# A two-layer decoder trunk on one core: modulation sums on VectorE, negated attention scores, and the gate row applied at the accumulators

## The chip, the cores and the metric

The kernel runs on one core of a Trainium2 chip. A core has TensorE (matmuls, into PSUM), VectorE, ScalarE, GpSimd and SyncE (which only issues transfers here); each works through its own queue in order. In the rows they are PE (and PEld for the loading of weights), DVE, ACT, POOL and SP. The metric is the device time of one execution in microseconds (us); less is better.

## The reference, cut to what matters

Two layers, 512 tokens, 1024 channels, all in f32. A layer is a modulated RMS norm, a token mixer, a residual add, a second modulated norm and a mixture of 16 experts with another residual add. The mixer of layer 0 is an mLSTM, that of layer 1 is differential attention with 8 heads.

```
c_act = silu(c)
mod = c_act @ w_ada[l] + b_ada[l]            # 1024 x 6144 per layer; sh1, sc1, g1, sh2, sc2, g2
h = rms(x, norm1[l]) * (1 + sc1) + sh1
y = mixer(h)                                  # projections, mixing, then @ w_out
x = x + g1 * y
...
# attention: for each head two score matrices of queries against keys
q = rope(rms(q, q_norm)) * 64 ** -0.5
p = softmax(where(mask, q @ k.T, -inf))       # p[0], p[1]
a = p[0] - lam * p[1]
```

## The kernel before, in words

Work is written as a program for each engine; a scheduler with a model of the times sets each engine's order before the run, save where the text ties it (`issue_after`, `ordered`). `later(n, fn)` puts work n steps ahead in a queue that `step()` runs.

**Modulation parts.** The 12 parts of `mod` (6 per layer) need w_ada, 4 MB per part. Layer 0's shift and scale for the first norm come from TensorE (`ada_half`). Six more parts, four of layer 0 and the first two of layer 1, come from `ada`, interleaved with the first mixer's projections: each part is four 1 MB transfers into a ring of four buffers (tag `raw`) that the projection weights share. A transfer holds two row blocks of 128 x 1024. Of a part's eight blocks the first is scaled on ScalarE (L255). In layer 0's parts blocks 2, 4 and 6 are multiplied and added in one VectorE operation (L257). All others are scaled in place on ScalarE (L259) and added on GpSimd (L260). `column_sums` then turns the sum (PE L301, DVE L302), and L307 writes `mod`. The last four parts of layer 1 use TensorE (`ada_rows`, L280).

**Weights in two parts.** Each projection weight block is split: a rounded high part on ScalarE (L228) and the low rest on VectorE (L229); for the first strips of the two mixers, `qk0` and `b00`, the rest is made on GpSimd. Every product is three TensorE matmuls. There are two buffers for low parts and three for high ones.

**Output projection.** `out_proj` runs for tokens 0 to 255 (half 0), then 256 to 511 (half 1), over the same four w_out buffers. In half 0 each accumulator is multiplied by the gate row g1 (L499) and added to x (L500). In half 0 GpSimd also multiplies each weight block by g1 in place (L512), after its split, and half 1 splits the product, so half 1 only adds. After `out_proj` of half 1 comes the route to the experts (squares, L366/L367, transposes, router logits L1087, ranks), then the experts, whose weights arrive in 1 MB transfers.

**Scores.** `scores` (L905 on) makes one 128-query block of one head: two matmuls (L917), a VectorE operation that adds the mask and takes the row maximum (L920), a tiny VectorE product with -0.125 (L923), the exponential on ScalarE (L924), the reciprocals and the factor of the second matrix (L927, L928), its scaling (L929) and the sum (L930).

**From layer 0 to layer 1.** The last expert's result is added to x by L1616, eight operations for the four token blocks. `normed_T` of layer 1 squares x on ScalarE (L373) and takes 1/rms from L366 on VectorE and L367 on GpSimd.

## Time and profile before

| what | value |
|---|---|
| median of 3 runs | 1228.6 us (1227.84 to 1230.41) |
| profiled execution | 1225.23 us |
| its span | 1223.4 us |
| TensorE busy | 1126.9 us, 92% |
| VectorE busy | 808.9 us, 66% |
| ScalarE busy | 659.1 us, 54% |
| GpSimd busy | 307.7 us, 25% |
| mean granted TensorE clock | 0.952 |

The span is that of the profiled execution; 1.83 us of its time lie outside it. The busy share is a mean over stages: start and first mixer until about 257 us, the end of its output projection and the route until 310, the experts of layer 0 until 582, attention until about 880, its route until 945, and the experts of layer 1.

### The profile page before, as it was taken

What the parts mean: (1) busy time and instruction counts of PE and PEld (TensorE: products, weight loads), DVE (VectorE), ACT (ScalarE), POOL (GpSimd) and SP (SyncE); (2) the same over time, 40 slices, a digit from 0 to 9 for tenths busy, and PEclk for the clock granted to TensorE, in tenths of its full rate; (3) what the DMA queues carried; (4) which work ended last, traced back from release to release, by engine and by line L of the source; (5) the groups of instructions that cost most, each with busy time, mean ns of one, the idle gap of its engine ahead of it and who ended that gap; (6) DMA issues with size and microseconds to landing.
All of it is one profiled execution on the core that took longest, in us unless ns stands there. A gap on an engine that the chain in (4) does not pass through costs nothing.

```text
span 1223.4 us, 17320 instructions
## 1 busy us (share of the span) xinstructions
PE 1126.9 (92%) x5954; PEld 816.0 (67%) x5954; DVE 808.9 (66%) x1617; ACT 659.1 (54%) x1118; POOL 307.7 (25%) x245
## 2 busy tenths in 40 slices
PE   5999999988999999996899999978797999999976
PEld 3677777777787875332897877757586787774322
DVE  4566878887888995006856566675677899893024
ACT  3456675443788885112655555555553888883110
POOL 2555482462211111101211021223233211111100
PEclk8999999997999999998999999988896999999998
DMA  9788662195799999999124444411275899999994
GB/s 345 267 284 302 230 216 104 59 346 194 280 383 382 386 380 368 398 408 370 37 70 141 138 169 138 173 69 74 99 280 193 316 386 385 377 380 372 396 414 182
DMA packets 104172, 320.81 MB, mean 262 GB/s; under 512 B 12673, under 2 KB 25097, under 8 KB 103056
## 3 DMA queue, kind: packets, MB, share of 16 engines
q1 hardware_dynamic: 95120, 298.67, 65.8%
q0 software_dynamic: 8960, 20.99, 4.7%
q8 instruction: 49, 0.80, 0.3%
q14 instruction: 43, 0.35, 0.1%
HBM read 309.66 MB, written 20.97 MB: 270 GB/s over the span
## 4 chain that ended last, share of the span: by engine, by line
PE 70%; DMA 12%; DVE 11%; ACT 4%; issue 2%; POOL 1%; SPq 0%; DVEq 0%; POOLq 0%; ACTq 0%
PE pge L237 8%; PE pue L237 8%; PE pge L1339 6%; PE po L237 6%; DMA we<-in_moe_w_gu_dram 5%; DMA ada<-in_w_ada_dram 5%; PE py0e L237 4%; PE py1e L237 4%; PE pye L1366 3%; PE s L917 3%; PE pcf L1398 2%; PE o L949 2%; PE xTe L427 1%; PE rowada L280 1%; PE psr L1087 1%
## 5 line engine op out<-in xcount | busy, mean ns | idle before, releaser
L1339 PE MATMUL pge<-we,xfe 128*64 128x512 f32 x448 | 106.3, 616 | 19.2 <-DMA we<-in_moe_w_gu_dram 19.2
L260 POOL TENSOR_TENSOR acc<-acc,ada 128x1024 f32<-128x1024 f32 x30 | 80.8, 2694 | 54.8 <-ACT ada L259 22.2
L1348 DVE TENSOR_TENSOR acte<-acte,pge 128x256 f32<-128x256 f32 x14 | 5.9, 421 | 119.3 <-ACT acte L1347 119.3
L1311 POOL DMA_INDIRECT xg<-h2d,lstd x26 | 26.8, 1031 | 223.0 <-PE xTe L427 152.5
L1339 PEld LDWEIGHTS pge<-we,xfe 128*64 128x64 f32 x448 | 30.4, 141 | 74.4 <-issue 51.1
L367 POOL TENSOR_TENSOR qrs<-qrs,nhalf 128x4 f32<-128x4 f32 x32 | 35.5, 1111 | 154.9 <-DVE qrs L366 126.5
L1366 PE MATMUL pye<-we,aTe 128*64 128x512 f32 x224 | 50.6, 593 | 1.1 <-ACT aTe L1355 1.1
L259 ACT ACTIVATE ada<-ada,cact 128x1024 f32<-128x1024 f32 x30 | 33.8, 1145 | 31.0 <-DMA ada<-in_w_ada_dram 31.0
L924 ACT ACTIVATE p<-p,mx 128x128 f32<-128x128 f32 (+3 forms) x64 | 35.7, 559 | 23.7 <-DVE mx L923 23.6
L920 DVE CUSTOM_DVE_ANT_0 p<-s,maskW 128x128 f32<-128x128 f32 (+3 forms) x64 | 30.4, 487 | 26.6 <-ACT orow L951 14.3
L512 POOL TENSOR_TENSOR wo<-wo,grow 128x1024 f32<-128x1024 f32 x16 | 40.9, 2573 | 23.6 <-DVE wos102l L229 15.8
L1347 ACT ACTIVATE acte<-pge 128x256 f32<-128x256 f32 x14 | 5.4, 383 | 73.1 <-PE pge L1339 73.1
L917 PE MATMUL s<-kTb,qTb 64*128 64x128 f32 (+3 forms) x128 | 40.1, 503 | 2.9 <-DVE mx L920 2.2
L1366 PEld LDWEIGHTS pye<-we,aTe 128*64 128x64 f32 x224 | 16.0, 137 | 32.3 <-issue 29.6
L427 PE MATMUL xTe<-ident,xg 128*128 128x128 f32 x144 | 23.0, 290 | 5.8 <-POOL we L220 3.2
L1463 POOL DMA_INDIRECT yd<-yoe,lstd x12 | 14.7, 1227 | 52.0 <-ACT yoe L1558 51.3
L949 PE MATMUL o<-vb,aTs 128*128 128x128 f32 x160 | 26.1, 303 | 0.7 <-ACT aTs L941 0.7
L1378 ACT ACTIVATE yo<-pye,twins 128x512 f32<-128x512 f32 x8 | 5.5, 687 | 38.9 <-PE pye L1366 38.9
L367 POOL TENSOR_TENSOR ors<-ors,nhalf 128x2 f32<-128x2 f32 (+1 forms) x12 | 11.2, 930 | 58.8 <-DVE mx L923 39.5
L949 PEld LDWEIGHTS o<-vb,aTs 128*128 128x128 f32 x160 | 23.2, 214 | 3.0 <-ACT aTs L941 1.6
L1379 POOL DMA_INDIRECT yd<-yo,rows x8 | 8.0, 1001 | 65.7 <-ACT yo L1378 65.4
L427 PEld LDWEIGHTS xTe<-ident,xg 128*128 128x128 f32 x144 | 18.5, 149 | 8.2 <-issue 6.0
(2557 smaller groups left out, 3871.5 us busy)
## 6 DMA issues: line engine op xcount, KB each, us to landing
we<-in_moe_w_gu_dram SPq DMA_DIRECT2D x128, 1024.0 KB, 8.7
we<-in_moe_w_down_dram SPq DMA_DIRECT2D x64, 1024.0 KB, 8.9
ada<-in_w_ada_dram SPq DMA_DIRECT2D x48, 1024.0 KB, 5.5
we<-yd SPq DMA_DIRECT2D x8, 1024.0 KB, 18.3
wo<-in_a_w_out_dram SPq DMA_DIRECT2D x4, 1024.0 KB, 4.9
wo<-in_b_w_out_dram SPq DMA_DIRECT2D x4, 1024.0 KB, 4.9
x<-in_x_dram SPq DMA_DIRECT2D x4, 512.0 KB, 5.0
qk0w<-in_a_w_in_dram SPq DMA_DIRECT2D x2, 1024.0 KB, 14.7
```

What stands on the lines that cost most here:

```text
L237: T.matmul(ps, (xh, xh, xl)[i], w, start=first and i == 0, stop=last and i == 2)
L259: A.activation(raw[:, k], raw[:, k], AF.Copy, scale=cact[:, kt:kt + 1])
L260: G.tensor_tensor(acc, acc, raw[:, k], op=ALU.add)
L367: pows.append(G.tensor_tensor(r, r, nhalf[:, 0:ncol], op=ALU.pow))
L427: T.transpose(ps[:, k * P:(k + 1) * P], row[:, kt * P:(kt + 1) * P], ident)
L512: G.tensor_tensor(raw[:, k], raw[:, k], grow, op=ALU.mult)
L917: T.matmul(ps[:, 0:n], part(qTs, h)[q0:q0 + BHD, j * P:(j + 1) * P], part(kTs, h)[q0:q0 + BHD, 0:n], start=True, stop=True)
L920: V.tensor_tensor_reduce(p[:, 0:n], ps[:, 0:n], maskW[:, S - n:S], scale=1.0, scalar=NEG, op0=ALU.add, op1=ALU.max, accum_out=mx[:, cc:cc ...
L924: A.activation(p[:, 0:n], p[:, 0:n], AF.Exp, scale=0.125, bias=mx[:, cc:cc + 1], accum_out=mx[:, 2 + cc:3 + cc])
L949: T.matmul(po[:, 0:P], aT[:, kb * P:(kb + 1) * P], part(vs, h)[:, kb * P:(kb + 1) * P], start=kb == 0, stop=kb == j)
L1339: T.matmul(pgu[hf * CS:(hf + 1) * CS].rearrange("p (g c) -> p g c", g=2), x[:, kt], w[:, :, hf], start=kt == 0, stop=kt == NK - 1))
L1366: T.matmul(py[hf * CS:(hf + 1) * CS], aT[:, k, ch * CS:(ch + 1) * CS], w[:, 0, hf * 512:(hf + 1) * 512], start=ch + k == 0, stop=ch + k == 2))
```

## The change

- `ada`: every row block but the first is one VectorE operation (L257's form); the ScalarE scaling and the GpSimd add are gone (30 of each).
- `strip`: the low parts of `qk0` and `b00` are made on VectorE.
- `out_proj`: GpSimd no longer multiplies w_out by the gate row (8 operations per layer); both halves multiply the accumulators by it on VectorE (4 operations more per layer).
- Scores: the factor -0.125 goes into the column `wcq` that scales q, so the scores are negated, the mask and the maximum change sign, L923 is gone, and L929 and L930 become one operation.
- Layer seam: the additions of L1616 keep program order, and for token blocks 2 and 3 of layer 1 the VectorE step of 1/rms (L366) is queued behind the last addition.

```diff
--- before.py
+++ after.py
@@ -211,7 +211,7 @@
         G.iota(slot, pattern=[[1, P]], base=0, channel_multiplier=0, **ints)
 
 
-    loads, last, act_last = [], [], []
+    loads, last, act_last, added = [], [], [], []
 
     def load(src, a, n, name, where=None, after=None):
         pool, tag, bufs = where or (raws, "raw", N_RAW)
@@ -253,11 +253,8 @@
                 kt = ch * 2 + k
                 if kt == 0:
                     A.activation(acc, raw[:, k], AF.Copy, scale=cact[:, kt:kt + 1])
-                elif k == 0 and l == 0:
+                else:
                     V.scalar_tensor_tensor(acc, raw[:, k], cact[:, kt:kt + 1], acc, op0=ALU.mult, op1=ALU.add)
-                else:
-                    A.activation(raw[:, k], raw[:, k], AF.Copy, scale=cact[:, kt:kt + 1])
-                    G.tensor_tensor(acc, acc, raw[:, k], op=ALU.add)
             if ch == 3:
                 room[2].append(lambda: ada_sums(l, j, acc))
                 later(3, lambda: room[2] and room[2].pop()())
@@ -371,7 +368,8 @@
 
         ss = small.tile([P, 1], F32, tag="ss", name=f"ss{l}{t}", bufs=4)
         A.activation(junk, xt[t], AF.Square, accum_out=ss)
-        r = rstd_of(ss, 1, D, f"r{l}{t}")
+        with tc.issue_after(added[0].ins) if added and t > 1 else nullcontext():
+            r = rstd_of(ss, 1, D, f"r{l}{t}")
         ps = [bank(f"hT{l}{t}{hf}") for hf in range(2)]
         for kt in range(NK):
             T.transpose(ps[kt // 4][:, kt % 4 * P:(kt % 4 + 1) * P], xt[t][:, kt * P:(kt + 1) * P], ident)
@@ -440,7 +438,7 @@
             raw = load(wk(w[k0 * P:(k0 + 2 * a) * P, col0:col0 + n]), 2 * a, n, f"{name}w{k0}",
                        first and first[k0 // (2 * a)])
             for k in (0, a):
-                yield k0 + k, split(raw[:, k:k + a], a, n, f"{name}s{k0 + k}", G if name in ("qk0", "b00") else V)
+                yield k0 + k, split(raw[:, k:k + a], a, n, f"{name}s{k0 + k}")
                 next(mix, None)
 
     def proj_rows(at, w, col0, evac, name, mix, n=512, by_token=False):
@@ -495,8 +493,7 @@
             if kt == NK - 1:
                 for n in range(2):
                     cols = slice(n * 512, (n + 1) * 512)
-                    if half == 0:
-                        V.tensor_tensor(ps[t, n], ps[t, n], grow[:, cols], op=ALU.mult)
+                    V.tensor_tensor(ps[t, n], ps[t, n], grow[:, cols], op=ALU.mult)
                     V.tensor_tensor(xt[t][:, cols], xt[t][:, cols], ps[t, n], op=ALU.add)
                 done(t)
             step()
@@ -508,8 +505,6 @@
             for k in range(2):
                 kt = ch * 2 + k
                 parts[kt] = split(raw[:, k:k + 1], 1, D, f"wos{l}{half}{kt}")
-                if half == 0:
-                    G.tensor_tensor(raw[:, k], raw[:, k], grow, op=ALU.mult)
                 if kt < NK - 3:
                     for t in ts:
                         products(t, kt)
@@ -834,6 +829,8 @@
             V.memset(wc, 1.0)
             for c0 in (0, BHD):
                 SP.dma_start(wc[c0 + R2:c0 + BHD], w[0:1, R2:].rearrange("o d -> d o"))
+            if nm == "q":
+                V.tensor_scalar(wc, wc, -0.125, None, op0=ALU.mult)
             tab = const.tile([P, NT, 2 * R2], F32, name=f"tab{nm}")
             bc = lambda a: a[:, None, :].to_broadcast([P, NT, ROPE_HALF])
             V.tensor_tensor(tab[:, :, 0:8], cos, bc(wr[:, 0:8]), op=ALU.mult)
@@ -864,7 +861,7 @@
             maskW = pool.tile([P, S], F32, name="maskW")
             G.memset(maskW[:, 0:S - P], 0.0)
             past(maskW[:, S - P:])
-            V.tensor_scalar(maskW[:, S - P:], maskW[:, S - P:], 0.0, NEG, op0=ALU.is_gt, op1=ALU.mult)
+            V.tensor_scalar(maskW[:, S - P:], maskW[:, S - P:], 0.0, -NEG, op0=ALU.is_gt, op1=ALU.mult)
             a1 = scale_of(1, slice(0, 4)) + scale_of(1, slice(4, 8))
             rows = [y_tile(f"rrow1{i}") for i in range(2)]
             for t in range(NT):
@@ -917,17 +914,15 @@
                     T.matmul(ps[:, 0:n], part(qTs, h)[q0:q0 + BHD, j * P:(j + 1) * P], part(kTs, h)[q0:q0 + BHD, 0:n],
                              start=True, stop=True)
                     p = pool.tile([P, S], F32, tag=f"p{cc}", name=f"p{j}{h}{cc}", bufs=3)
-                    V.tensor_tensor_reduce(p[:, 0:n], ps[:, 0:n], maskW[:, S - n:S], scale=1.0, scalar=NEG,
-                                           op0=ALU.add, op1=ALU.max, accum_out=mx[:, cc:cc + 1])
+                    V.tensor_tensor_reduce(p[:, 0:n], ps[:, 0:n], maskW[:, S - n:S], scale=1.0, scalar=-NEG,
+                                           op0=ALU.add, op1=ALU.min, accum_out=mx[:, cc:cc + 1])
                     pr.append(p)
-                    V.tensor_scalar(mx[:, cc:cc + 1], mx[:, cc:cc + 1], -0.125, None, op0=ALU.mult)
-                    A.activation(p[:, 0:n], p[:, 0:n], AF.Exp, scale=0.125, bias=mx[:, cc:cc + 1],
+                    A.activation(p[:, 0:n], p[:, 0:n], AF.Exp, scale=-1.0, bias=mx[:, cc:cc + 1],
                                  accum_out=mx[:, 2 + cc:3 + cc])
                 p0, p1 = pr
                 V.reciprocal(mx[:, 4:6], mx[:, 2:4])
                 V.scalar_tensor_tensor(mx[:, 5:6], mx[:, 5:6], mx[:, 2:3], nlam, op0=ALU.mult, op1=ALU.mult)
-                V.tensor_scalar(p1[:, 0:n], p1[:, 0:n], mx[:, 5:6], None, op0=ALU.mult)
-                V.tensor_tensor(p0[:, 0:n], p0[:, 0:n], p1[:, 0:n], op=ALU.add)
+                V.scalar_tensor_tensor(p0[:, 0:n], p1[:, 0:n], mx[:, 5:6], p0[:, 0:n], op0=ALU.mult, op1=ALU.add)
                 later(5, lambda: probs_T(j, h, p0, mx))
 
             def probs_T(j, h, p0, mx):
@@ -1613,7 +1608,8 @@
                     to_tokens(banks[t], t, *mine, False, True)
                     for hf in range(2):
                         x = xt[t][:, hf * 512:(hf + 1) * 512]
-                        V.tensor_tensor(x, x, banks[t][hf], op=ALU.add)
+                        added[:] = [V.tensor_tensor(x, x, banks[t][hf], op=ALU.add)]
+                        ordered(added[0])
             elif e >= NE - NSEL:
                 selected.append((weighted_few(py, e), places(e)))
             elif e == NE - NSEL - 1:
```

## Rows read from the trace of the kernel before

**Rows 1.** Stages: us, busy of each engine (instructions), PEclk, DMA share, GB/s
```profile
50.00:222.00 172.00, 164.72 (x771) 130.85 (x769) 128.70 (x223) 103.38 (x162) 85.86 (x38) 1.00 0.61 211
222.00:257.00 35.00, 28.50 (x152) 23.57 (x151) 30.55 (x39) 14.11 (x24) 24.36 (x11) 0.95 0.51 196
...
600.00:790.00 190.00, 189.17 (x1412) 155.91 (x1411) 118.80 (x449) 101.61 (x277) 35.40 (x33) 1.00 0.39 134
790.00:880.00 90.00, 74.36 (x390) 55.75 (x389) 61.39 (x175) 50.20 (x134) 28.86 (x17) 0.85 0.25 94
```

**Rows 2.** The expert stage of layer 0, same view and columns
```profile
330.00:470.00 140.00, 139.69 (x642) 110.91 (x641) 126.07 (x125) 117.86 (x138) 24.13 (x20) 1.00 1.01 380
```

**Rows 3.** Groups of instructions, POOL, 20 to 300 us (busy, mean ns, idle before)
```profile
L260 POOL TENSOR_TENSOR acc<-acc,ada 128x1024 f32<-128x1024 f32 x30 | 80.8, 2694 | 54.8 <-ACT ada L259 22.2 <-DVE acc L257 15.2 <-PE o0p L456 5.1
```

**Rows 4.** Groups of instructions, DVE, 28 to 282 us
```profile
L257 DVE SCALAR_TENSOR_TENSOR acc<-ada,cact,acc 128x1024 f32<-128x1024 f32 x12 | 15.4, 1280 | 11.8 <-DMA ada<-in_w_ada_dram 6.5 <-POOL acc L260 5.4
```

**Rows 5.** Timeline of DVE and PE, first mixer: start, us, idle before
```profile
140.68 3.43 DVE L229 TENSOR_TENSOR v1s2l<-v1w,v1s2h 128x1024 fp32r<-128x1024 f32 x1
...
257.32 1.21 DVE L229 TENSOR_TENSOR wos011l<-wo,wos011h 128x1024 fp32r<-128x1024 f32 x1
...
144.16 0.50 PE L455 MATMUL v1p<-v1s2l,ah 128*128 128x512 f32 x1 [1.07 <-DVE v1s2l L229]
```

**Rows 6.** Timeline of POOL, DVE and PE, end of the first mixer
```profile
234.03 21.09 POOL L512 TENSOR_TENSOR wo<-wo,grow 128x1024 f32<-128x1024 f32 x8 [1.21 <-ACT grow L361]
...
240.21 3.38 DVE L229 TENSOR_TENSOR wos007l<-wo,wos007h 128x1024 fp32r<-128x1024 f32 x1
...
244.25 0.66 PE L427 MATMUL ht<-ident,hrow 128*128 128x128 f32 x4 [2.15 <-DVE cs L302]
250.69 1.12 PE L360 MATMUL psrow<-ident,a 128*128 128x128 f32 x4 [3.68 <-DVE swr L1030]
```

**Rows 7.** Timeline of POOL, DVE and PE, end of attention
```profile
814.11 5.24 POOL L512 TENSOR_TENSOR wo<-wo,grow 128x1024 f32<-128x1024 f32 x2
...
814.59 2.56 DVE L891 TENSOR_TENSOR qrow<-qrow,qrs 128x256 f32<-128x256 f32 x1
...
817.19 2.21 DVE L894 TENSOR_TENSOR rot<-qrow,tabk 128x32 f32<-128x32 f32 x1
...
860.60 2.40 DVE L928 SCALAR_TENSOR_TENSOR mx<-mx,nlam 128x1 f32<-128x1 f32 x1
...
820.16 0.66 PE L903 MATMUL qkT<-ident,qrow 128*128 128x128 f32 x2 [4.71 <-DVE mx L928]
...
864.30 1.06 PE L917 MATMUL s<-kTb,qTb 64*128 64x256 f32 x2 [2.19 <-DVE mx L920]
```

**Rows 8.** Groups of instructions, DVE, 600 to 880 us
```profile
L891 DVE TENSOR_TENSOR qrow<-qrow,qrs 128x256 f32<-128x256 f32 x32 | 15.6, 488 | 7.7 <-POOL qrs L367 6.5 <-PE qkT L903 1.2
...
L929 DVE TENSOR_SCALAR p<-p,mx 128x128 f32<-128x128 f32 (+3 forms) x32 | 12.3, 386 | 0.8
...
L923 DVE TENSOR_SCALAR mx<-mx 128x1 f32<-128x1 f32 x64 | 8.4, 147 | 0.3
```

**Rows 9.** Timeline of DVE, last additions of layer 0's projection
```profile
282.47 1.88 DVE L500 TENSOR_TENSOR x<-x,po 128x512 f32<-128x512 f32 x3 [0.60 <-PE po L237]
284.27 1.33 DVE L229 TENSOR_TENSOR guse01l<-we,guse01h 128x1024 fp32r<-128x1024 f32 x1
285.53 0.67 DVE L500 TENSOR_TENSOR x<-x,po 128x512 f32<-128x512 f32 x1
```

**Rows 10.** Timeline of DVE, the seam between the layers
```profile
582.22 0.15 DVE L366 TENSOR_SCALAR r<-ss 128x1 f32<-128x1 f32 x1 [1.27 <-ACT sq L373]
```

**Rows 11.** Timeline of DVE and PE, start of the first projection
```profile
24.74 2.23 DVE L398 TENSOR_SCALAR a<-mod 128x4 f32<-128x4 f32 x1
...
28.46 2.07 PE L479 MATMUL qk0p<-ah,qk0s0h 128*128 128x512 f32 x4 [0.23 <-ACT ah L403]
```

**Rows 12.** Waits of ACT, 50 to 222 us: total us, times, longest
```profile
ACT ada L259 <- DMA ada<-in_w_ada_dram: 22.7, 12, 3.2
```

## The prediction, made before the change was run

> **What bounds the kernel now.** I read the table of stages first, to find where TensorE is idle, then the timelines of TensorE and VectorE at each idle place, then what GpSimd did at that moment.
>
> In the main part of the first mixer TensorE is busy for 164.72 of 172.00 us, and through attention for 189.17 of 190.00 [rows 1]. Work taken from other engines there is mostly work that TensorE already covers. The idle time lies in two short stretches: 6.50 us in the 35 us from 222 to 257, and 15.64 us in the 90 us from 790 to 880 [rows 1]. In the expert stage behind them TensorE is busy for 139.69 of 140 us while the transfers run at a DMA share of 1.01 [rows 2]. Its work starts when the route has chosen the tokens, so I expect what is won before it to shift the rest as a whole.
>
> The timelines show what ends the idle time. A low part takes VectorE 1.21 us when GpSimd is quiet and 3.43 us when it is not, and TensorE then waits 1.07 us for it [rows 5]. For the 21.09 us in which GpSimd multiplies the eight w_out blocks, a low part takes 3.38 us, and TensorE stands for 2.15 and 3.68 us behind small VectorE work that is queued after it [rows 6]. Near the end of attention it is the same: beside two GpSimd products of 5.24 us in all, two VectorE operations take 2.56 and 2.21 us, the second on 32 elements per partition, and TensorE stands for 4.71 us; later one on a single element takes 2.40 us, and TensorE stands for 2.19 us [rows 7]. So GpSimd costs this kernel time by holding up VectorE, not by its own results.
>
> The Trainium skill says why (GPSIMD Engine Reference, Specifications): GpSimd's SBUF interfaces are shared with VectorE, and they contend when a VectorE instruction has two SBUF inputs or runs in a two-port mode. By that rule the added operations, with two SBUF inputs each, also wait whenever GpSimd works, which speaks against them. Beside the GpSimd work that the rows leave in the main part (85.86 us less 28 of the 30 removed adds at 2.694, some 10 us) that would put up to 10 us on VectorE, and the sum would be 10 us smaller if all of it reached TensorE; the trace agrees with the rule itself (2.40 us on one element, in an operation with several inputs), not with such a price, since TensorE's gaps are much shorter than VectorE's stretches.
>
> **The change part by part.** The sum is made against the profiled execution, 1225.23 us (its span 1223.4 and 1.83 around it). The median of the runs is 1228.6, which is 3.37 higher.
>
> *Start of the first projection.* The `qk0` low part held VectorE's 4-element operation for 2.23 us, just ahead of the first projection [rows 11]. But TensorE was on a modulation matmul until 0.23 us before that projection starts [rows 11], and I expect it to keep that order. Bounds: nothing, and the 2.23. I take -0.2, the gap.
>
> *Modulation in the main part.* Removed: 30 GpSimd adds of 2.694 us [rows 3] and 30 ScalarE scalings. Added: 30 VectorE operations at 1.280 [rows 4], 38.4 us, two of them before 50 us. VectorE is busy for 128.70 of 172 us there [rows 1]. With nothing given back it would be at about 165, full; if half of 28 adds stretched an operation by the 2.22 us between 3.43 and 1.21 [rows 5], 31 us come back and it is at 133, as full as before. I take that half, as an estimate. TensorE's idle time in this part is 7.28 us in all [rows 1], so no more can be won; the one gap shown of this cause is 1.07 [rows 5]. I take -2.0, about two such gaps. The other bound is a loss, from waits on the w_ada transfers that move into VectorE's queue, ahead of the low parts that TensorE needs: ScalarE waited 22.7 us for them, in 12 waits [rows 12]. One wait holds up a low part less than the other buffer covers: a block of 1024 columns feeds 24 matmuls, and a release of the buffers no longer waits for GpSimd. So I take no loss.
>
> *Gate row, layer 0.* The eight products of 21.09 us are gone [rows 6]. TensorE's two gaps are 5.83 us together [rows 6], of 6.50 idle in the stretch [rows 1]. Each ends behind VectorE work that was stretched. I take -5.5; bounds nothing and -6.5.
>
> *Gate row, layer 1.* The same eight products go. Of the gap of 4.71 us the two operations at their usual length (0.49 for the first form, mean of 32 [rows 8]) leave about 0.5, so 4.2 come back; the gap of 2.19 goes with the stretch of 2.40 [rows 7]. That is -6.4, and I take -6.5 with the small stretches around. Bounds: -2.2 if only one of the two comes back, and -11, two thirds of the idle 15.64 [rows 1].
>
> *Half 1's four gate products, per layer.* Three additions of a 128x512 accumulator take 1.88 us, 0.63 each [rows 9]; a product of the same shape is priced alike. The last addition now ends at 286.20 (285.53 and 0.67). Eight operations from 282.47 on end at 287.5 if the split of 1.33 us that lies between [rows 9] is put elsewhere, and at 288.8 if not: 1.3 to 2.6 later. Some of it is hidden, since token block 3 queues behind the logits of block 2. I take +1.0 per layer, +2.0; bounds 0 and 5.2.
>
> *Scores.* 64 operations of 147 ns and 32 of 386 ns go [rows 8], 21.7 us of VectorE. Up to 790 us TensorE hides all of it: 0.83 us idle in 190 [rows 1]. If that cover were gone it would be worth up to those 21.7. From 790 on each pair of score blocks has a chain shorter by some 0.5 us, mostly beside other heads. I take -0.5; bounds nothing and -3.
>
> *Seam of the layers.* The additions of block 3 no longer stand behind a 1/rms step that waits 1.27 us for ScalarE [rows 10]. Their accumulators were done only shortly before, so not all of it counts: -0.4; bounds nothing and -1.3. Behind it waits the ScalarE square of block 3. The low parts of `b00` go to VectorE at the end of layer 0, where it is idle: nothing, or +2.4, two at 1.21, if the weighted sum of the last expert is queued behind.
>
> Sum: -0.2 - 2.0 - 5.5 - 6.5 + 2.0 - 0.5 - 0.4 = -13.1. That is 1212.1 us for an execution like the profiled one, and 1215.5 against the median.
>
> **The rivals.**
>
> *VectorE's queue takes the mixer's gain back.* The waits on w_ada stand ahead of the low parts, just enough to cost what the removal of GpSimd's work wins in layer 0. For it: the mixer has 38.4 us more of VectorE work. Against it: GpSimd no longer stretches it. Only layer 1, the seam and the scores count: -6.5 - 0.5 - 0.4 + 2.0 = -5.4, 1223.2 us.
>
> *Slower: VectorE bounds the first mixer.* All 22.7 us of waits [rows 12] move to VectorE and reach TensorE, and the 2.0 of the main part is not won: 1228.6 - 11.1 + 22.7 = 1240.2 us. It decides from 11.1 us on, when half of those waits reach TensorE. For it: at 165 of 172 us VectorE would have no room for them. Against it: ScalarE stood in these waits, made the high parts in the same queue, and TensorE was idle for only 7.28 us.
>
> *Nothing comes of it.* Other waits (ScalarE's copies, the ring of four buffers) end in the same places as the stretched VectorE work: 1228.6 us.
>
> *More comes of it.* All the idle time goes that GpSimd's work could have caused: -7.3 in the main part, -6.5 behind it, -11 at the end of attention, -2 in seam and scores, nothing lost in half 1: -26.8, 1201.8 us.
>
> **How the numbers follow.** Forecast, 1215.5 us: 0.55; its own range is 1209 to 1221, by the bounds of the two gate terms. Gain in layer 1 alone, 1223.2: 0.20. Slower, 1240.2: 0.10. Nothing, 1228.6: 0.07. More, 1201.8: 0.08. Faster by over 0.2% (2.5 us, about what a measurement of this kernel can tell from no change) is 0.55 + 0.20 + 0.08 = 0.83; within it 0.07; slower 0.10. For a range of 8 in 10 I leave out most of the case of more and the slower case: 1205 to 1228.
>
> **What would show it.** Right: no VectorE operation of 2 to 3.5 us beside GpSimd in 222 to 257 and 810 to 866, where TensorE's gaps of 2.15, 3.68, 4.71 and 2.19 us are gone; VectorE busy for about 130 of 172 us in the main part, and TensorE no more idle there; the experts of layer 0 starting some 7 us earlier and those of layer 1 some 13. Wrong: gaps of TensorE behind low parts that wait for a w_ada operation; the four gaps still there behind other work; a last addition of half 1 more than 2.6 us later behind its last matmul than now.

## The result, and the profile after

The changed kernel takes 1219.24 us (median) where the kernel before takes 1229.47: a ratio of 0.990, 95% interval 0.9868 to 0.9932. Run again beside the experiments it took 1215.58 against 1227.51, 0.9904 (0.9876 to 0.9932). The forecast was 1215.5, faster, with a range of 1205 to 1228. The first profiled execution of the changed kernel took 2186.41 us, with matmuls of nearly twice the usual length throughout (1140 ns for 616 in the experts' first product), so the profile after is that of the second measurement (one execution of 1215.05 us, span 1212.9).

I cut both profiles into stages at the same events, read from TensorE's timeline: the first and last matmul of the output projection (`po`), the first transposed expert input (`xTe`), the last matmul of the combination (`pcf`), the first of `b00`, the last of `bv6`. The first fence is the kernel before: first mixer, output projection of layer 0, its tail up to the experts; then the last heads of attention, the output projection of layer 1, its tail. Columns as in [rows 1].

```profile
28.46:211.94 183.48, 175.65 (x819) 135.99 (x820) 127.39 (x217) 106.38 (x158) 94.73 (x53) 0.99 0.68 238
211.94:283.83 71.89, 65.39 (x340) 54.21 (x339) 58.97 (x101) 32.85 (x54) 32.87 (x21) 0.98 0.55 205
283.83:308.31 24.48, 16.14 (x95) 15.50 (x93) 17.74 (x76) 7.25 (x13) 8.61 (x10) 0.58 0.39 148
808.00:836.20 28.20, 17.70 (x96) 13.15 (x95) 17.66 (x46) 16.78 (x42) 6.92 (x4) 0.72 0.11 38
836.20:920.11 83.91, 76.64 (x376) 60.50 (x375) 58.05 (x131) 43.99 (x101) 30.04 (x20) 0.91 0.46 176
920.11:943.23 23.12, 14.66 (x95) 13.94 (x93) 17.40 (x75) 7.16 (x13) 8.42 (x9) 0.63 0.52 198
```

The same six stages of the changed kernel:

```profile
28.29:207.58 179.29, 175.36 (x823) 137.88 (x820) 130.46 (x250) 79.09 (x130) 8.06 (x20) 0.98 0.68 244
207.58:270.71 63.13, 63.13 (x338) 52.94 (x336) 48.14 (x101) 32.37 (x54) 11.22 (x12) 1.00 0.57 226
270.71:298.64 27.93, 17.93 (x96) 16.90 (x95) 19.82 (x79) 7.31 (x13) 9.53 (x10) 0.59 0.41 147
801.40:822.95 21.55, 16.04 (x89) 11.10 (x87) 11.85 (x36) 15.18 (x36) 1.70 (x2) 0.81 0.13 49
822.95:900.56 77.61, 74.02 (x374) 58.53 (x372) 49.05 (x113) 43.39 (x101) 13.67 (x13) 0.94 0.49 190
900.56:928.90 28.34, 18.10 (x95) 17.19 (x95) 20.09 (x81) 6.98 (x13) 8.38 (x9) 0.55 0.42 162
```

The first column after the window is the length; length less PE's busy time is TensorE's idle time. Subtracted, with what the prediction gave for the stage:

```
stage                        change   of it idle   of it TensorE busy   predicted
first mixer                   -4.2       -3.9             -0.3            -2.0
output projection, layer 0    -8.8       -6.5             -2.3            -5.5
tail, layer 0                 +3.5       +1.7             +1.8            +1.0
last heads of attention       -6.7       -5.0             -1.7   } -6.5 and
output projection, layer 1    -6.3       -3.7             -2.6   } -0.5 (scores)
tail, layer 1                 +5.2       +1.8             +3.4            +1.0
```

In the two output projections and the two tails TensorE's instructions are the same in both kernels, but for one or two at the edges. There the idle time that went took TensorE busy time with it, and the idle time that came brought some: the matmuls themselves ran faster or slower. In the last heads it is otherwise. Seven instructions fewer stand in that stage (89 for 96), since the scheduler put them ahead of the end of `bv6`, and they account for the 1.7 us of busy time.

The other stages: start -0.2 (predicted -0.2), experts of layer 0 +1.1, seam (end of `pcf` to `b00`) 6.43 to 7.30, +0.9 (predicted -0.4), attention up to `bv6` +1.1 (it holds those seven instructions), experts of layer 1 274.1 to 278.9, +4.8. The sum of all is -9.5 between the two profiles, up to the last matmul of the combination; the spans differ by 10.5. The experts of layer 0 start 9.7 us earlier and those of layer 1 14.3, where the prediction said some 7 and 13.

What answers to the rows of before. The low part of w_out that took 3.38 us in [rows 6], and the small operation behind it:

```profile
232.74 1.23 DVE L229 TENSOR_TENSOR wos007l<-wo,wos007h 128x1024 fp32r<-128x1024 f32 x1 [0.63 <-PE po L237]
...
234.95 0.17 DVE L304 TENSOR_TENSOR mod<-cs,vcol 128x8 f32<-128x8 f32 x1
```

The gaps of 2.15, 3.68, 4.71 and 2.19 us [rows 6, 7] have no counterpart; from `po` first to `po` last in layer 0 TensorE is busy for 63.13 of 63.13 us. Two VectorE operations of 2.3 us are left in that stage beside GpSimd's L1062 (at 247.82 and 251.88); TensorE waits for neither. The 30 GpSimd adds [rows 3] are gone, and the VectorE group of [rows 4] has 42 members of the same length; its waits for w_ada total 7.3 us:

```profile
L257 DVE SCALAR_TENSOR_TENSOR acc<-ada,cact,acc 128x1024 f32<-128x1024 f32 x42 | 53.9, 1282 | 9.6 <-DMA ada<-in_w_ada_dram 7.3 <-ACT acc L255 1.9 <-DVE wcq L829 0.2
```

New is a wait at the start of the first mixer, where two of these operations stand ahead of the modulation of the second half of the input, and one more ahead of its low parts:

```profile
46.04 1.28 DVE L257 SCALAR_TENSOR_TENSOR acc<-ada,cact,acc 128x1024 f32<-128x1024 f32 x1
...
47.36 1.28 DVE L257 SCALAR_TENSOR_TENSOR acc<-ada,cact,acc 128x1024 f32<-128x1024 f32 x1
...
48.56 1.91 DVE L408 TENSOR_SCALAR xnT<-xnT,a,mod 128x512 f32<-128x512 f32 x4
...
50.67 1.28 DVE L257 SCALAR_TENSOR_TENSOR acc<-ada,cact,acc 128x1024 f32<-128x1024 f32 x1 [0.19 <-DVE wcq L829]
...
51.87 2.49 DVE L402 TENSOR_TENSOR al<-xnT,ah 128x512 fp32r<-128x512 f32 x4
...
49.82 1.72 PE L477 MATMUL qk0p<-ah,qk0s4h 128*128 128x512 f32 x4 [2.27 <-ACT ah L401]
...
52.61 0.80 PE L478 MATMUL qk0p<-al,qk0s4h 128*128 128x512 f32 x1 [0.64 <-DVE al L402]
...
53.20 0.63 PE L479 MATMUL qk0p<-ah,qk0s4l 128*128 128x512 f32 x1
...
53.63 0.63 PE L477 MATMUL qk0p<-ah,qk0s4h 128*128 128x512 f32 x1
...
50.00:57.00 7.00, 6.36 (x15) 4.30 (x16) 6.81 (x14) 2.61 (x4) 0.63 (x4) 0.52 0.63 180
```

TensorE waits 2.27 us, and then its 128x512 matmuls are issued 0.43 us apart. The granted clock from 50 to 57 us is 0.52, the lower level (1.2 of 2.4 GHz) nearly throughout. VectorE's small additions and memsets between them are left out of the fence. The kernel before starts these matmuls 0.23 us apart, at the full clock:

```profile
50.00:57.00 7.00, 7.00 (x32) 5.19 (x30) 6.77 (x9) 3.62 (x5) 5.16 (x4) 1.00 0.54 120
```

In the tail of layer 1 a split of the first expert's weights stands among half 1's products (L496) and additions (L497), and the last addition ends 5.3 us behind the last `po` matmul, where it was 2.4 before ([rows 9] show the additions of layer 0, also 2.4). What follows on TensorE, first in the changed kernel:

```profile
901.60 1.92 DVE L229 TENSOR_TENSOR guse01l<-we,guse01h 128x1024 fp32r<-128x1024 f32 x1
...
904.04 1.87 DVE L497 TENSOR_TENSOR x<-x,po 128x512 f32<-128x512 f32 x3
...
904.77 1.12 PE L1070 MATMUL x2T<-ident,x 128*128 128x128 f32 x4 [2.98 <-DVE x L497]
...
905.96 1.97 PE L1070 MATMUL x2T<-ident,x 128*128 128x128 f32 x8
...
907.72 1.73 PE L1082 MATMUL psr<-awr,x2T 128*128 128x16 f32 x8
...
905.00:912.00 7.00, 6.99 (x38) 6.83 (x37) 6.82 (x20) 4.11 (x8) 3.65 (x5) 0.50 0.68 274
```

and in the kernel before:

```profile
922.55 1.09 PE L1075 MATMUL x2T<-ident,x 128*128 128x128 f32 x8 [1.51 <-DVE x L500]
...
923.48 0.96 PE L1087 MATMUL psr<-awr,x2T 128*128 128x16 f32 x8
...
922.50:926.00 3.50, 3.23 (x30) 3.14 (x30) 3.46 (x8) 2.98 (x6) 3.03 (x3) 0.99 1.02 405
```

The eight transposes of a token block take 1.97 us where they took 1.09, the eight logit matmuls 1.73 where they took 0.96: after a wait of 2.98 us in place of 1.51 TensorE does the same work at a granted clock of 0.50 in place of 0.99.

### The profile page after: what moved, and what is told of

The parts are those of the page before. It is cut to its first block, busy times and chain, and to the rows that moved or that the text cites. A ratio compares the mean times of both kernels' runs of the same rounds, so it can differ in the third digit from the quotient of the medians.

```text
span 2184.5 us, 17129 instructions
## 1 busy us (share of the span) xinstructions
PE 2145.9 (98%) x5954; PEld 1308.0 (60%) x5954; DVE 799.9 (37%) x1566; ACT 651.8 (30%) x1090; POOL 164.3 (8%) x193
## 4 chain that ended last, share of the span: by engine, by line
PE 97%; DVE 1%; DMA 1%; ACT 1%; issue 0%; POOL 0%; SPq 0%; DVEq 0%; POOLq 0%; ACTq 0%
PE pge L1334 10%; PE pge L237 9%; PE pue L237 9%; PE po L237 8%; PE pye L1361 5%; PE py0e L237 5%; PE py1e L237 5%; PE s L914 3%; PE pcf L1393 2%; PE o L944 2%; PE xTe L425 2%; PE rowada L277 1%; PE psr L1082 1%; PE aT L934 1%; PE aTe L1440 1%; PE qk0p L478 1%
## 5 line engine op out<-in xcount | busy, mean ns | idle before, releaser
L1334 PE MATMUL pge<-we,xfe 128*64 128x512 f32 x448 | 213.2, 1140 | 0.0
L1361 PE MATMUL pye<-we,aTe 128*64 128x512 f32 x224 | 108.0, 1158 | 1.1 <-ACT aTe L1350 1.1
L1361 PEld LDWEIGHTS pye<-we,aTe 128*64 128x64 f32 x224 | 22.4, 188 | 80.1 <-issue 78.3
L914 PE MATMUL s<-kTb,qTb 64*128 64x128 f32 (+3 forms) x128 | 62.8, 800 | 0.6 <-ACT kTb L901 0.6
L257 DVE SCALAR_TENSOR_TENSOR acc<-ada,cact,acc 128x1024 f32<-128x1024 f32 x42 | 53.8, 1281 | 6.2 <-ACT acc L255 5.7
L1393 PE MATMUL pcf<-yo,self 64*128 64x512 f32 x96 | 45.4, 1140 | 1.7 <-DVE yo L1367 1.7
L425 PE MATMUL xTe<-ident,xg 128*128 128x128 f32 x144 | 40.2, 442 | 5.8 <-POOL we L220 3.2
L944 PE MATMUL o<-vb,aTs 128*128 128x128 f32 x160 | 44.0, 456 | 0.5 <-ACT aTs L936 0.5
L944 PEld LDWEIGHTS o<-vb,aTs 128*128 128x128 f32 x160 | 40.3, 345 | 6.6 <-issue 4.6
L277 PE MATMUL rowada<-ada,acc 128*32 128x512 f32 x128 | 33.6, 1087 | 0.0
L1082 PEld LDWEIGHTS psr<-awr,x2T 128*128 128x128 f32 x128 | 30.6, 361 | 1.3 <-issue 0.9
```

What stands on the lines that cost most here:

```text
L257: V.scalar_tensor_tensor(acc, raw[:, k], cact[:, kt:kt + 1], acc, op0=ALU.mult, op1=ALU.add)
L277: T.matmul(ps[at:at + 32], cp[:, ch * 2 + k], raw[:, k, hf * 512:(hf + 1) * 512], start=True, stop=True)
L425: T.transpose(ps[:, k * P:(k + 1) * P], row[:, kt * P:(kt + 1) * P], ident)
L914: T.matmul(ps[:, 0:n], part(qTs, h)[q0:q0 + BHD, j * P:(j + 1) * P], part(kTs, h)[q0:q0 + BHD, 0:n], start=True, stop=True)
L944: T.matmul(po[:, 0:P], aT[:, kb * P:(kb + 1) * P], part(vs, h)[:, kb * P:(kb + 1) * P], start=kb == 0, stop=kb == j)
L1082: T.matmul(ps, xT[:, kt], awr[:, kt], start=kt == 0, stop=kt == NK - 1)
```

## The experiments

**The whole change, and two parts of it.** All ten hunks; the gate row alone (the deletion of GpSimd's products and the `if half == 0` of out_proj); the modulation alone (the hunk of `ada`).

Whole change. 

> The changed kernel once more, for a profile in the usual state. Theory (GpSimd costs time by holding up VectorE): 0.985 to 0.993 of before; none of the TensorE gaps of 2.15, 3.68, 4.71 and 2.19 us is left, no VectorE operation of 2 to 3.5 us stands beside the output projections, the first mixer's main part has VectorE at some 130 of 172 us. Rival (VectorE's queue takes the mixer's gain back): the experts of layer 0 start less than 2 us earlier, and new TensorE gaps end behind low parts that waited for a modulation operation.

Measured above: 0.9904.

Gate row alone. 

> Before, with only the gate row moved to the accumulators in both halves. Theory: 7 to 12 us faster than before (5.5 + 6.5 - 2.0 = 10), most of the whole gain. Rival (gain comes from the modulation sums): within 3 us of before.

0.9927 (0.9899 to 0.9955), 1218.0 us. Its stages: output projection of layer 0 63.1, tail 27.8, last heads 23.4, output projection of layer 1 75.5, tail 28.1. So all that layer 1 wins, and the longer tails, belong to the gate row; the last heads lack 1.8 us that the whole change has, and its output projection is 2.1 us shorter.

Modulation alone. 

> Before, with only the modulation row blocks as VectorE operations. Theory: 0 to 4 us faster, TensorE was idle for only 7.28 us in that part. Rival (VectorE bounds the mixer): 5 us or more slower. Rival (the modulation carries the gain): 6 us or more faster.

0.9992 (0.9976 to 1.0007): no change that can be told. The first mixer is 1.6 us shorter (181.9), the tail of layer 0 1.3 (23.2; a second profile of the kernel before, below, shows the same 23.3), and the output projection of layer 1 is 3.1 longer (87.0; why is open). The loss at the start of the mixer is there too, and larger: waits of 2.66 and 1.27 us, and the fourth weight block (`qk0s6`) starts at 61.36, where it starts at 55.60 before and at 59.86 in the whole change.

**Is it the products, or who makes them?** In layer 0, half 0, GpSimd multiplies the eight w_out blocks by the gate row again, into a buffer that nothing reads at that time (`spare` holds it in that half alone); half 1 still multiplies at the banks.

```diff
...
                 parts[kt] = split(raw[:, k:k + 1], 1, D, f"wos{l}{half}{kt}")
+                if spare:
+                    G.tensor_tensor(spare[0], raw[:, k], grow, op=ALU.mult)
...
```

> The whole change, and in layer 0 alone GpSimd multiplies each of the eight w_out blocks by the gate row again, into a buffer that nobody reads at that time; this is work added, whose result is not used. Theory (contention, not the result): the gain of layer 0's output projection is lost, 4 to 7 us slower than the whole change, with VectorE operations of 2 to 3.5 us there and TensorE gaps behind them; layer 1 keeps its gain. Rival (it was the wait for the product in half 1, a dependency): no slower than the whole change by more than 1 us, since nothing waits for this result.

0.9986 (0.9967 to 1.0005), 1226.4 us: work whose result is not used takes back all of the gain, some 10 us, more than I expected. The output projection of layer 0 takes 74.4 us (63.1 in the whole change). GpSimd, VectorE and TensorE:

```profile
247.05 2.37 POOL L510 TENSOR_TENSOR xg<-wo,grow 128x1024 f32<-128x1024 f32 x1
...
261.36 2.38 POOL L510 TENSOR_TENSOR xg<-wo,grow 128x1024 f32<-128x1024 f32 x1
...
247.06 3.43 DVE L229 TENSOR_TENSOR wos011l<-wo,wos011h 128x1024 fp32r<-128x1024 f32 x1
...
259.82 5.01 DVE L229 TENSOR_TENSOR wos013l<-wo,wos013h 128x1024 fp32r<-128x1024 f32 x1
...
270.49 2.32 DVE L1015 TENSOR_TENSOR eq<-eq,left 128x128 f32<-128x128 f32 x1
...
272.73 1.21 DVE L229 TENSOR_TENSOR wos015l<-wo,wos015h 128x1024 fp32r<-128x1024 f32 x1
...
250.55 1.22 PE L237 MATMUL po<-wos011l,h2h 128*128 128x512 f32 x2 [2.21 <-DVE wos011l L229]
...
274.00 0.92 PE L237 MATMUL po<-wos015l,h2h 128*128 128x512 f32 x2 [3.24 <-DVE wos015l L229]
```

The gap of 2.21 us ends behind a low part that took 3.43 us. The gap of 3.24 ends behind one that took its usual 1.21, but stood behind a small operation of 2.32 (0.28 in the kernel before). None of these VectorE operations has a data dependence on GpSimd, and VectorE waits for a GpSimd result only once in the stage, for 0.73 us, as in the whole change (0.74). So contention is enough for the loss, and the rival of a dependence falls.

The rows also show of what kind the contention is: a held operation does not run slower, it runs later. `wos011l` ends at 250.49, 1.07 us behind the GpSimd product that ends at 249.42; `wos013l` ends at 264.83, 1.09 behind the one that ends at 263.74. In this profile 15 VectorE operations took over 0.4 us longer than the shortest of their form beside a GpSimd operation. All 15 end behind the end of a GpSimd operation by that shortest length less 0.12 to 0.19 us. It goes the other way too: `wos015l` got in between two products, and those two take 6.17 us together, where two others take 4.87.

**The kernel before once more.** 

> The kernel before once more, for a second profile of it. In its first profile the expert stage of layer 1 (from the first transposed expert input, 943.23, to the last matmul of the combination, 1217.3) took 274.1 us, and in the four kernels run since it took 277.3 to 278.9. Theory: the first profiled execution was 3 to 4 us quick there, which is also why its 1225.23 lies below the median of 1228.6; this one takes 277 to 279 in that stage and 1227 to 1229 in all. Rival: the stage of the kernel before does take 274, and every edit tried since loses 4 us in it; then this one shows 274 again and the whole change hands 4 us back there.

1225.13 us; the experts of layer 1 took 275.7. That is 1.6 more than in the first profile and still below the 276.4 to 278.9 in the profiles of all eleven other kernels of this study. Part of the +4.8 is the spread of executions; whether 1 or 2 us are lost there stays open. The other stages agree with the first profile within 0.8 us, but for the tail of layer 0: 23.3 in place of 24.5. Against this profile the whole change loses 4.7 us in that tail, not 3.5.

**VectorE makes the products, in half 0.**

```diff
...
-                    V.tensor_tensor(ps[t, n], ps[t, n], grow[:, cols], op=ALU.mult)
+                    if half == 0:
+                        V.tensor_tensor(ps[t, n], ps[t, n], grow[:, cols], op=ALU.mult)
...
+                if half == 0:
+                    V.tensor_tensor(raw[:, k], raw[:, k], grow, op=ALU.mult)
...
```

> The whole change, but in half 0 VectorE (not GpSimd) multiplies each of the eight w_out blocks in place by the gate row, behind its low part, and half 1 only adds, as before. Theory: half 1's four products at the banks cost 3.4 us in layer 0 and 5.2 in layer 1 in the whole change (last matmul of the output projection to first transposed expert input: 24.5 to 27.9, 23.1 to 28.3), and it was GpSimd beside VectorE, not the product itself, that made the old place expensive. Then these two stages come back to about 24.5 and 23.5, the eight products of about 1.2 us each fit beside TensorE (VectorE is busy for 17.7 of 25 us at 220 to 245), and the time is about 8 us below the whole change, 1207 to 1209. Rival: 9.8 us more of VectorE work in half 0 of each layer holds up the low parts that TensorE needs, by 2 to 5 us per layer in the time from the first to the last matmul of the output projection: 1212 to 1216, no gain over the whole change. Second rival: the longer stage has another cause than the products; it stays at 27.9 and 28.3, 1215 to 1219.

0.9884 (0.9857 to 0.9910), 1215.26 us: the first rival. The tails come back, to 23.1 and 22.9 us, so their price is that of half 1's products; but the output projection of layer 0 goes from 63.13 to 70.82, since eight more VectorE operations stand ahead of low parts and of the route's small work (one gap behind `wos007l` is 1.87 us). In layer 1 the last heads take 25.0 for 21.5 and the output projection 78.8 for 77.6:

```profile
209.34:280.16 70.82, 66.78 (x340) 55.57 (x339) 56.06 (x109) 32.57 (x54) 12.88 (x13) 0.95 0.55 208
...
919.71 1.09 PE L1073 MATMUL x2T<-ident,x 128*128 128x128 f32 x8 [1.50 <-DVE x L498]
...
920.64 0.96 PE L1085 MATMUL psr<-awr,x2T 128*128 128x16 f32 x8
```

The last two lines are the tail of layer 1: with a wait of 1.50 us the transposes take 1.09 again, and the logits 0.96.

**The split out of the tail.** The low parts `guse00` and `guse01` are ordered behind the last 1/rms step of the route.

```diff
...
-        on.tensor_tensor(lo, raw, hi.bitcast(F32), op=ALU.subtract)
+        with tc.issue_after(after.ins) if after else nullcontext():
+            on.tensor_tensor(lo, raw, hi.bitcast(F32), op=ALU.subtract)
...
-        V.tensor_scalar(r, src, 1.0 / count, EPS, op0=ALU.mult, op1=ALU.add)
+        tail[:] = [V.tensor_scalar(r, src, 1.0 / count, EPS, op0=ALU.mult, op1=ALU.add)]
...
+        ready = [split(fetch.ready[0][:, k:k + 1], 1, D, f"guse0{k}", after=tail[0]) for k in range(2)]
...
```

> The whole change, with the two first low parts of the experts (guse00, guse01) made to stand behind the last 1/rms step of the route in VectorE's queue. In the whole change the second of them lies among half 1's eight gate products and additions (271.75, 1.92 us, stretched by GpSimd). Theory: it delays the last addition and with it the route; without it the last addition ends 1.3 to 1.9 us earlier in each layer and the stage from the last matmul of the output projection to the first transposed expert input goes from 27.9 and 28.3 to about 26.3 and 26.7: 1211.5 to 1213. Rival: behind the 1/rms step the two low parts (2.5 us) stand ahead of the scaling of the tokens that the experts gather, and give the same back or more: 1214.5 to 1218.

0.9874 (0.9850 to 0.9897), 1212.3 us. The tails take 26.77 and 26.58 (27.93 and 28.34): -1.2 and -1.8, close to the 1.6 per layer of the theory. Against the whole change the intervals overlap, so this gain is shown by the stages and not by the time. In both layers waits of 0.57 and 1.14 us stand ahead of the last transposes here (the first is not in the fence), and what follows them differs, first in layer 0, then in layer 1:

```profile
274.47 0.66 PE L1071 MATMUL x2T<-ident,x 128*128 128x128 f32 x4 [1.14 <-DVE x L498]
...
275.67 1.09 PE L1071 MATMUL x2T<-ident,x 128*128 128x128 f32 x8 [0.38 <-DVE x L498]
...
902.07 1.12 PE L1071 MATMUL x2T<-ident,x 128*128 128x128 f32 x4 [1.14 <-DVE x L498]
...
903.27 1.97 PE L1071 MATMUL x2T<-ident,x 128*128 128x128 f32 x8
```

So the length of a wait does not by itself say at which level the matmuls behind it run.

**The modulation behind the input.**

```diff
...
+            al_last[:] = [in_parts(*channels(h, hf * 4 + k), x)]
...
+                    with tc.issue_after(al_last[0].ins):
+                        V.scalar_tensor_tensor(acc, raw[:, k], cact[:, kt:kt + 1], acc, op0=ALU.mult, op1=ALU.add)
...
```

> The whole change, with the modulation operations on VectorE (L257) ordered behind the last low part of the mixer's second input half. In the whole change two of them stand ahead of that half's modulation (46.04 and 47.36, 1.28 us each) and one more ahead of its low parts; TensorE waits 2.27 us at 49.82 and 0.64 at 52.61, its matmuls run at half clock until about 57, and the first matmul of the fourth weight block of the first projection starts at 59.86, against 55.60 before. Theory: this is a loss of about 4 us that the whole change takes at the start of the first mixer and mostly carries to its end; without it the output projection of layer 0 starts 2 to 4 us earlier (207.6 to about 204.5) and the time is 1212 to 1213.5. Rival: VectorE's queue or the transfers set the pace later in the mixer, the loss is made up anyway, and the order changes nothing: within 1 us of the whole change.

0.9819 (0.9796 to 0.9843), 1208.1 us, 10 us or 0.9% less than the whole change relative to the kernel before: the one single edit that is faster than the whole change with an interval apart from its. The output projection of layer 0 starts at 204.0 us (207.6), as the theory says, and the gaps of 2.27 and 0.64 us are gone. That shows 3.6 us; the rest of the difference lies in stages that this edit does not touch, its own profile (1212.09 us, the longest of its five) doesn't show it, and the whole change was not run beside it.

**Both orders together.** 

> The whole change with both of the last two edits: the modulation operations behind the last low part of the mixer's input, and the experts' two first low parts behind the route's last 1/rms step. Theory: the two losses lie in different stages (the start of the first mixer; behind the output projections) and add up. Relative to the kernel before of their own job, the whole change stood at 0.9904, with the first order at 0.9819, with the second at 0.9874, so both together give about 0.979, 1203 us where the kernel before takes 1229. Rival: what the earlier start wins is spent by waits that are there anyway behind it (transfers of the experts, the clock), and both together are no better than the first alone, 0.982.

0.9830 (0.9801 to 0.9859), 1207.2 us. Not told apart from the order of the modulation alone, so the time doesn't show the sum. The stages do: output projection of layer 0 at 203.1 (4.5 us earlier than in the whole change), tails of 26.95 and 26.65 (1.0 and 1.7 shorter). These 7.2 us account for most of the 9 us between the two ratios. At the start of the mixer:

```profile
50.57 1.29 DVE L404 TENSOR_TENSOR al<-xnT,ah 128x512 fp32r<-128x512 f32 x2
...
51.77 2.60 DVE L259 SCALAR_TENSOR_TENSOR acc<-ada,cact,acc 128x1024 f32<-128x1024 f32 x2
...
55.17 0.86 PE L479 MATMUL qk0p<-ah,qk0s6h 128*128 128x512 f32 x3
```

The modulation operations come behind the last low parts, and the fourth weight block of the first projection (`qk0s6`) starts at 55.17; in the whole change it starts at 59.86, in the kernel before at 55.60.

**The same without the scores edit.** The three hunks of the scores undone in it. 

> The kernel with both orders, with the scores of the second mixer as in the kernel before (positive scores, a separate scaling of the maximum, two operations to join the two maps; 96 VectorE operations more). Theory: the shorter scores are worth nothing, and they cost a little: with them TensorE waits about 1.8 us at 737 for the split of the weight block b06, a wait that the kernel before and the kernel with the gate row alone don't have; without them attention (first matmul of its first projection to the last of its last, 220.8 in the whole change) takes 219 to 220 and the time is within 0.2% of both_orders or 1 to 2 us below. Rival, as predicted: the shorter scores save 0.5 us or more at the end of attention, and this kernel is 0.5 to 3 us slower than both_orders.

1205.1 us, 0.9819 (0.9789 to 0.9849): not slower without the edit. The edit moves time about, and no gain of it can be told from the time: with it the last heads take 21.55 us, without it 23.14; the output projection of layer 1 takes 77.48 with it and 75.62 without, at granted clocks of 0.94 and 0.98. The wait for `b06` (at 737 us in the whole change, 1.78 us at 732.5 with both orders) is gone without it. But attention up to `bv6` took 222.2 us without it and 221.2 with it, the other way than I expected; over the three stages together the two profiles differ by 0.7 us, in favour of the edit.

**The same without the seam edit.** The additions of block 3 and the 1/rms step in their old order. 

> The kernel with both orders, with the seam of the layers as before: the additions of token block 3 are not put ahead of the 1/rms step of block 2. Theory: the seam edit wins what it was priced at or a little more, since from the last matmul of the combination to the first of b00 it took 6.5 us before and 5.9 to 6.0 in the two kernels with one order (7.3 in the whole change itself): this kernel shows 6.4 to 6.5 there and is 0.5 us slower, not to be told from both_orders by the time. Rival: the first additions of block 3 lie ahead of work that TensorE needs first, which made the 7.3; then this kernel is 0.5 to 1.5 us faster.

1209.5 us, 0.9847 (0.9821 to 0.9874). From the end of `pcf` to `b00` it takes 6.44 us, with the edit 5.99: the 0.5 of the theory, by the stage; the times are not apart.

**The scores alone.** 

> The kernel before with the scores edit alone. Theory: within 0.15% of the kernel before (0.9985 to 1.0015), with the same gaps of TensorE at the end of attention (4.7 and 2.2 us), since these come from GpSimd's products beside VectorE and the edit leaves both. Rival: the edit shortens VectorE's chain between the scores and the turned maps, and the 96 operations that go away make room beside GpSimd: 1.5 to 3 us faster, 0.9975 to 0.9988.

0.9997 (0.9973 to 1.0022), 1227.6 us, an interval too wide to tell 1.5 us from nothing. In the trace the theory falls, as far as one profile shows it (1221.87 us, the shortest of its twelve): beside GpSimd's products the edit does shorten VectorE's queue, the gap of 4.71 us [rows 7] is down to 1.61:

```profile
817.52 0.66 PE L905 MATMUL qkT<-ident,qrow 128*128 128x128 f32 x2 [1.61 <-DVE mx L928]
```

and the last heads and the output projection behind them take 25.3 and 80.9 us, 2.9 and 3.0 less than before. So the scores edit and the gate row edit remove the same stall: what one of them takes away the other finds gone.

## Why the prediction was right, and where its sum was not

The direction, the forecast and its main cause held. GpSimd costs by what it does to VectorE: shown by the products whose result nothing uses. That is the rule of the Trainium skill (GPSIMD Engine Reference, Specifications) weighed in the prediction, and the trace agrees: a two-input low part takes 1.21 us alone and 3.28 to 5.01 beside them. That the added operations would suffer by it, up to 10 us, is not seen: 42 of them at 1.28 us, none above 1.29. The rule was not put to the test on them, though: only two of the 42 ran beside GpSimd work, copies of one element, and there GpSimd was held (1.20 and 1.26 us for 0.18). The sum of -13.1 stands against -11.9 by the medians (1227.51 less 1215.58), and -10.2 in the first measurement. That it came so close is in part luck: terms of both signs were too small. By the stages the gains are some 11.5 us larger than summed, and against them stand 15.0 us of losses that were too small or not in the sum (tails, experts, seam, attention).

- *Gate row, -5.5 and -6.5.* Mis-sized: -8.8, and with the scores -13.0. I priced each gap at its length. The idle time that went is 6.5 and 8.7 us. Of the further 2.3 and 4.3 us of busy time, 2.3 and 2.6 are matmuls of the output projections that ran faster; the 1.7 of the last heads are the instructions that moved ahead of the stage, so that the -13.0 is -11.9 with attention counted in. My bound of -11 was called two thirds of the idle 15.64, which is 10.4. The granted clock of the kernel before around and behind the gaps that end at 250.69, 820.16 and 864.30 [rows 6, 7]:

```profile
249.00:254.00 5.00, 3.31 (x12) 2.79 (x13) 5.00 (x8) 0.60 (x1) 5.00 (x3) 0.66 1.02 409
820.00:828.00 8.00, 5.24 (x26) 4.20 (x26) 4.96 (x18) 5.22 (x13) 0.69 (x1) 0.71 0.00 0
860.00:870.00 10.00, 6.24 (x22) 4.26 (x24) 7.50 (x22) 5.35 (x17) 2.35 (x1) 0.72 0.39 154
```

 0.66, 0.71 and 0.72, against 1.00 from the first to the last matmul of the output projection of layer 0 in the changed kernel.
- *Half 1's gate products, +2.0.* Mis-sized in the same way, outside its bounds of 0 and 5.2: +8.7 (10.0 against the second profile of before). In each layer 3.0 us of it is VectorE's queue (eight operations and the split among them), a little over my upper bound of 2.6 per layer; a last addition more than 2.6 us later was one of the signs that I had named as wrong, and it came. In layer 1 the rest is the transposes and logits at half clock: 0.88 for the transposes, 0.77 and 0.83 for the logits (1.73 and 1.87 for 0.96 and 1.04). With the products elsewhere all of it goes.
- *Main part, -2.0.* -4.2 in the stage, and some 4 us more were there to win: with the modulation ordered behind the input the stage takes 175.5, and 175.2 with both orders (203.06 less 27.87), -8.3. I had set the idle time of 7.28 us as the limit. The loss is the wait that I looked for in the wrong place: not a low part behind a w_ada transfer, but the input's own modulation behind added operations. I had counted two of these ahead of 50 us and given them no price. The modulation alone gives 1.6 us in this stage (0.9 against the second profile of before) and nothing that the time shows. What of the -4.2 belongs to the low parts of `qk0`, which that run leaves on GpSimd, was not tried.
- *Scores, -0.5.* Nothing to be told, as the stages of attention cover it and one stage pays for the other.
- *Seam, -0.4.* With an order edit the stage fits (5.98 to 6.00 for 6.43); in the whole change it is 0.9 longer. But the event misleads there: `b00` starts later and then runs through, where in the kernel before it stops for 2.23 us.

```profile
580.56 0.58 PE L452 MATMUL b00p<-b00s0h,bh 128*128 128x256 f32 x1 [0.21 <-DVE xnT L381]
```

```profile
590.99 0.39 PE L454 MATMUL b00p<-b00s0h,bh 128*128 128x256 f32 x1 [2.23 <-ACT bh L403]
```

 The first line is of the whole change, the second of the kernel before. From the end of `pcf` to the end of the last `b00` matmul it is 22.0 us for 22.4, the -0.4 of the sum; but kernels with the seam edit range from 21.7 to 23.0 there and those without from 22.4 to 23.3, so the size is not shown.
- *Start, -0.2.* 28.46 to 28.29, but the kernel before has 28.71 in its second profile, and kernels with this edit range from 27.9 to 29.3: not to be told. The low parts of `b00` at nothing: not tried alone, and neither was the start.

*More comes of it* was nearer in some stages than in its sum: the idle time went as it said in the output projection of layer 0 (6.5 us), nearly so at the end of attention (8.7 of 11), and by half in the main part (3.9 of 7.3). *VectorE bounds the first mixer* did not happen: VectorE was busy for 130 of 179 us, and of the w_ada waits 7.3 us are left. What takes the excess back in the whole change is the tails (8.7) and, in these two profiles, the experts of layer 1 (4.8).

The best version measured is the change with the modulation operations behind the input: 0.982 to 0.985, 1205 to 1210 us in four variants that the time does not tell apart.

## What to carry to other kernels

A gap of TensorE is priced at its length plus the matmuls behind it that run at the lower granted clock: here 10.2 us of idle time in the output projections took 4.9 us of busy time with it, and 3.4 us of new idle time in the tails brought 5.2. The second part is a range and not a fixed rate, since equal waits were followed by either level. When work moves to an engine with room to spare, look at what its queue then puts ahead of the one result that the bounding engine waits for: the average (130 of 179 us) said nothing of the 4 us lost at the start. Work on GpSimd was off the path here only where the VectorE work beside it was too: an operation that comes second waits for the whole one that came first.

## What was not expected of the hardware

- How much a short wait can cost behind itself, and how little its length says of it. Eight transposes took 1.97 us behind a wait of 2.98 us and 1.09 behind one of 1.50 in the same place. But behind waits of 0.58, 1.14 and 0.37 us they took 1.97 with both orders, and behind 0.57, 1.14 and 0.38 they took 1.09 in the same kernel without the scores edit. What decides stays open.
- GpSimd's product of a 128x1024 block took VectorE's two-input operation of the same size from 1.21 to as much as 5.01 us, by making it wait for whole GpSimd operations, two of them back to back in that case.
- The granted clock can fall where TensorE hardly idles: in the profile with the modulation behind the input it was 0.89 in one stretch of 30 us of attention (TensorE busy for 29.22; it fell behind a wait of 0.58 us), 1.00 in the same stretch of the whole change (29.72). Executions go with it: of the twelve of the scores alone, the slowest (1236.48 us) had a mean granted clock of 0.941 and the fastest (1221.87) 0.954: 14.6 us between two executions of one kernel, more than the whole change gains.

```profile
701.00:731.00 30.00, 29.22 (x179) 21.99 (x179) 16.00 (x59) 15.04 (x48) 6.88 (x6) 0.89 0.25 88
```
